# Weight loads and gate stores begun by ScalarE instead of SyncE, in a two-layer conv, mLSTM and latent-attention block

## The chip, the cores and the metric

The kernel runs on one NeuronCore of a Trainium2 chip. The core has a matrix engine (TensorE, PE in the profile, with its weight loads as PEld), a vector engine (VectorE, DVE), an engine for activations (ScalarE, ACT), a general one (GpSimd, POOL) and SyncE (SP), which computes nothing and here begins the DMA transfers. Each engine takes its own instructions strictly in order and waits on semaphores for the others. Every DMA runs on the same 16 DMA engines, whoever began it. The metric is the time of one execution on the device, in microseconds (us); 0.2% of it is about 5 us.

## What is computed

Two layers of a block with three branches over 512 tokens of width 1024 and 256 context tokens; the last layer needs the 512 tokens alone. In short:

```python
u = x * (1 + sc1) + sh1                       # modulation: silu(c) @ w_mod + b_mod, six parts
a, qkv, o_pre, g_if, cq, ckv, kr, gates = split(u @ w_in + b_in)   # the context likewise
y_conv = silu(layer_norm(depthwise_conv31(val * sigmoid(gate)))) @ w_conv_out
y_ml   = (sigmoid(o_pre) * norm(mlstm_bidirectional(q, k, v, g_if))) @ w_mlstm_out  # chunks of 128
y_mla  = attention(latent queries, latent keys and values, rope) @ w_mla_out        # 8 heads
g_a, g_b, g_c = split(sigmoid(gates))
y = (g_a * y_conv + g_b * y_ml + g_c * y_mla) @ w_out + b_out
x = layer_norm(alpha * x + g1 * y)
x = layer_norm(alpha * x + g2 * (relu(x' @ w1 + b1) ** 2 @ w2 + b2))   # x' modulated again
```

All numbers are float32.

## The kernel before, in words

Activations lie features by tokens: eight tiles of 128 x 768 (512 tokens and 256 of the context; 512 in the last layer). A product of float32 precision is made of three matmuls of a narrower float32 kind (fp32r): every operand is split into a high part (the rounded value) and a low part (the rest), and `mm3` (L265 to L268) adds high x high, high x low and low x high in PSUM. L268 is the only one of the three that reads a weight's low part. `gemm` (L279) runs this over the 128-row blocks of one weight tile; its result lies in one of two PSUM buffers (pg), and is taken out by ScalarE or VectorE.

A weight tile is 128 x 1024 (512 KB), up to 1152 wide. `wload` (L256) loads it into a buffer wr, ScalarE casts it to the high part wh (L261), and VectorE, or GpSimd for the gates and the output gate, subtracts to make the low part wl (L262). Each of wr, wh and wl has three buffers. So the load of tile i needs the wr buffer of tile i-3, free when that tile's low part is made, and the cast of tile i needs the wh buffer of tile i-3, free when its last matmul has run. `plan` (L201) lists the tiles of the whole kernel in the order of use, 328 of them, and `wget` (L249) hands out the next and calls `ahead` (L242), which keeps two more staged (LOOK = 2).

The stages of a layer: the convolution's inputs and its 31 taps on VectorE (L494), woven into what follows; value and gate columns (L536 to L538); the scans for the mLSTM's gates; keys and queries; the mLSTM chunk by chunk in both directions (`mstep`, with the decay weights loaded by L662 from a copy in DRAM, m_dram); the three branches' gates (24 tiles, L757 to L779), each put through tanh by ScalarE (L760) and stored to z_dram by L779; meanwhile pieces of the next modulation (`mod_pieces`, L151), whose w_mod tiles are loaded by L160, summed on VectorE (L165, into mda) and transposed by TensorE (L173). Then `merge` for the convolution and the mLSTM, which reloads each gate (`mload`, L76, into ml), multiplies it with the product (L803) and stores it again (L807); the latent projections; attention (scores, exponentials, transposes L982, values L1003); the third merge (L1065); w_out in token groups of 256 columns (L1103), whose residual comes by L1091 and is added in L1104, each group followed by a layer normalization (`ln_fm`: transposes L314 and L336, scaling L326) with its outputs L1080 to L1083; and the feed-forward part in eight blocks, where w1's results go through L1126 to L1129 and w2's are added in L1139. At the start, `first_loads`, `first_mods`, `first_u`, `first_w` and `first_gemm` (L360 to L399) weave the first modulation's w_mod loads (L130), the inputs' loads (L364) and three tiles of w_in; TensorE's order is written out by hand there alone.

Elsewhere the builder sets each engine's order when the program is built: it plans the instructions on assumed durations, by the order in which the code makes them and by when their operands and buffers are free. An edge of the kind `tc.add_manual_dep(..., NOSYNC)` only fixes an order and adds no wait on the chip where both instructions are on one engine. The builder puts in the semaphores as well. Before the change every DMA of the kernel is begun by SyncE, in one queue.

Of the kernel before, what the change touches and what calls it, by code (L numbers as in the profile page):

```python
# [14 lines left out]
NOSYNC = mybir.DependencyInfo(mybir.DependencyClass.NoSync, mybir.DependencyReason.DATA)  # L15
# [29 lines left out]
def build(tc, I, out):  # L45
    nc = tc.nc
    V, A, G, PE = nc.vector, nc.scalar, nc.gpsimd, nc.tensor
# [10 lines left out]
    def slot(name, dt=F32):  # L58
        return gp.tile([128, T], dt, name=name, tag="s")
# [13 lines left out]
    def mload(src):  # L73
        n = src.shape[1]
        t = mp.tile([128, 512], F32, name="ml", tag="m")
        nc.sync.dma_start(t[:, :n], src)  # L76
        return t[:, :n]
# [164 lines left out]
    def ahead(k):  # L242
        while len(staged) < k:
            p = next(todo, None)
            if p is None:
                return
            staged.append((p[0], wload(*p[1:])))

    def wget(*key, look=LOOK):  # L249
# [3 lines left out]
        ahead(look)  # L253
        return w

    def wload(src, n, eng):  # L256
        r = wp.tile([128, 1152], F32, name="wr", tag="wr")
        nc.sync.dma_start(r[:, :n], src)
        h = wp.tile([128, 1152], F32R, name="wh", tag="wh")
        lo = wp.tile([128, 1152], F32R, name="wl", tag="wl")  # L260
        A.copy(h[:, :n], r[:, :n])  # L261
        eng.tensor_sub(lo[:, :n], r[:, :n], h[:, :n])  # L262
        return h, lo

# [75 lines left out]
    def ln_fm(src, nk, groups, emit, base=0):  # L340
        for _ in ln_groups(src, nk, groups, emit, base):
            pass
# [3 lines left out]
    def pull(k):  # L346
        for _ in range(k):
            next(mods, None)
# [3 lines left out]
    z_dram = dp.tile([3, 8, 128, T], F32, name="z_dram")  # L352
# [100 lines left out]
    for l in range(L):  # L453
        full = l < L - 1
        n = T if full else S
# [44 lines left out]
        def some_taps(k):  # L500
            for _ in range(k):
                next(taps, None)

        for j in range(4):
# [5 lines left out]
            h = slot("hc")  # L510
# [15 lines left out]
        for hf, w_n in ((0, VG0), (1, VG1)):  # L526
            ws = [wget("w_vg", l, hf * 2 + q) for q in range(2)]
            for tt in range(NT):
                ps = pg()
                t0 = tt * 128  # L530
                for k in range(8):
                    wh, wl = ws[k // 4]
                    a, b = (k % 4) * w_n, (k % 4 + 1) * w_n
# [41 lines left out]
        for tt in range(NT):  # L575
            a, b = tt * 128, tt * 128 + 128
# [180 lines left out]
        def gate(b, mt):  # L757
            ps = win(MT_G + b * 8 + mt, n)
            t = slot("gt_")
            A.activation(t[:, :n], ps[:, :n], AF.Tanh, bias=HB(MT_G + b * 8 + mt), scale=0.5)  # L760
            return t
# [14 lines left out]
        for b in range(3):  # L776
            for mt in range(8):
                g = gate(b, mt)
                nc.sync.dma_start(z_dram[b, mt, :, :n], g[:, :n])  # L779
                some_taps(3)  # L780
                pull(2)
                if b * 8 + mt == 10:
                    some_taps(200)
                    ln_fm(ca, 4, groups, conv_emit)
# [105 lines left out]
        for hf in range(2):  # L890
            w = wget("w_ukv", l, hf)
            for tt in range(NT):
                ps = pg()
                t0 = tt * 128
                for k in range(2):
                    a, b = k * 512, (k + 1) * 512
# [21 lines left out]
        for hf in range(2):  # L918
            ws = [wget("w_uq", l, hf * 2 + q) for q in range(2)]
            for tt in qts:  # L920
                ps = pg()
                t0 = tt * 128
                for k in range(6):
                    wh, wl = ws[k // 3]
                    a, b = (k % 3) * 384, (k % 3 + 1) * 384
# [131 lines left out]
        for mp2 in range(4):  # L1057
            w = wget("w_ao", l, mp2)
            for i in range(2):
                mt = 2 * mp2 + i  # L1060
                ps = gemm(w, 4 * i, 4, oT, n)
                for (_, _, c0, c1), zz in zip(tg_, zg):
                    g = mload(z_dram[2, mt, :, c0:c1])
# [49 lines left out]
        for f in range(NF):  # L1113
            hid = []
            for j in range(FB):
                mt = f * FB + j
# [7 lines left out]
                r, hh, hl = slot("r"), slot("hidh", F32R), slot("hidl", F32R)  # L1124
# [7 lines left out]
            if f < NF - 1:  # L1132
                for mp2 in range(4):
                    w = wget("w2", l, f, mp2)
                    for i in range(2):
                        mt = 2 * mp2 + i
# [157 lines left out]
```

## Time and profile before

| | before |
|---|---|
| time, median of 3 runs | 2557.14 us (2556.3 to 2558.33) |
| the profiled execution's own time | 2557.35 us |
| its span, first to last instruction | 2555.5 us |
| mean granted TensorE clock | 0.993 |
| busy: TensorE, VectorE, ScalarE, GpSimd | 2470.4, 1580.6, 939.5, 298.7 us |
| DMA: all of it in one queue | 296.00 MB, 36.9% of 16 engines |
| mean rate over the span | 116 GB/s |

The profile is one execution. A row of its groups gives line, engine, operation, what is written and read, and how often; then the busy time, the mean of one in ns, and the engine's idle time just before, with what ended it. A row of waits gives who waited for whom: total us, times, longest. A row of windows gives a stretch of time, then the busy time of PE, PEld, DVE, ACT and POOL in it with counts, the granted clock as a share of full speed, the DMA engines' busy share and GB/s. A row of the timeline gives start, duration, engine (a q behind the name is its instruction queue), line, operation and tiles; neighbours of a kind are merged (x3), and a bracket holds the idle time before it and what ended it. DMA-issuing instructions do not count as busy time of an engine.

### The profile page before, as it was taken

Reading aid. Unit: us, or ns where it says so; the run is one execution under the profiler, and the core shown is the slowest. Engines: PE = TensorE matmul, PEld = TensorE weight load, DVE = VectorE, ACT = ScalarE, POOL = GpSimd, SP = SyncE. Lnnn points to the kernel's source line nnn. Section 1 sums busy time; section 2 is a strip of 40 time slices with the busy share of each in tenths; the row PEclk is TensorE's granted clock in tenths of the full one; section 3 lists DMA queues with packets and bytes.
Section 4 is the critical chain, followed back from the end, with each engine's and each line's share of the span. In section 5 each row is a group of like instructions: output and inputs, shape, how many; then the busy total and the mean of one; then the engine's idle time right before and its main releaser. Section 6 shows DMA issues by size and latency. Waiting matters only on the chain.

```text
span 2555.5 us, 38339 instructions
## 1 busy us (share of the span) xinstructions
PE 2470.4 (97%) x15272; PEld 2163.8 (85%) x15272; DVE 1580.6 (62%) x2847; ACT 939.5 (37%) x1607; POOL 298.7 (12%) x235
## 2 busy tenths in 40 slices
PE   7899989999999999999999999999999999999997
PEld 5888878888888899888888888977888888888887
DVE  4999976363356777655554379996043567554456
ACT  3123323222457563222222253333324575432323
POOL 0002132203000021000000031023411001100002
PEclk9999999999999999999999999999999999999999
DMA  7122344466110654343342252233563106333333
GB/s 264 53 75 70 98 163 161 166 195 210 62 34 1 188 168 142 122 131 115 108 129 88 65 149 78 59 106 101 175 203 111 50 18 213 101 99 92 99 94 113
DMA packets 137235, 298.45 MB, mean 117 GB/s; under 512 B 13776, under 2 KB 55248, under 8 KB 137056
## 3 DMA queue, kind: packets, MB, share of 16 engines
q1 hardware_dynamic: 137056, 296.00, 36.9%
q8 instruction: 120, 1.97, 0.3%
q14 instruction: 59, 0.48, 0.1%
HBM read 265.49 MB, written 30.46 MB: 116 GB/s over the span
## 4 chain that ended last, share of the span: by engine, by line
PE 81%; DVE 9%; DMA 4%; ACT 2%; issue 2%; POOL 1%; SPq 0%; DVEq 0%; ACTq 0%; POOLq 0%
PE pg L266 21%; PE pg L267 21%; PE pg L268 21%; PE pt L1003 2%; PE pt L982 2%; PE pt L266 2%; PE pt L267 2%; PE pt L268 2%; DVE ca L494 2%; DMA wm<-w_mod 1%; DMA ml<-z_dram 1%; PE pg L536 1%; PE pg L538 1%; PE pg L537 1%; DVE st L315 1%
## 5 line engine op out<-in xcount | busy, mean ns | idle before, releaser
L261 ACT CAST wh<-wr 128x1024 fp32r<-128x1024 f32 (+1 forms) x328 | 345.6, 1055 | 1202.4 <-PE pg L267 825.5
L262 DVE TENSOR_TENSOR wl<-wr,wh 128x1024 fp32r<-128x1024 f32 (+2 forms) x272 | 338.6, 1246 | 410.1 <-ACT wh L261 406.3
L268 PE MATMUL pg<-uh,wl 128*128 128x512 f32 (+1 forms) x1280 | 456.3, 356 | 2.2 <-DVE wl L262 2.2
L266 PE MATMUL pg<-uh,wh 128*128 128x512 f32 (+1 forms) x1280 | 457.2, 357 | 1.2 <-ACT gt__17278 L760 1.2
L267 PE MATMUL pg<-ul,wh 128*128 128x512 f32 (+1 forms) x1280 | 455.5, 356 | 0.7 <-POOL ul L1171 0.6
L266 PE MATMUL pg<-hidh,wh 128*128 128x512 f32 (+1 forms) x832 | 285.4, 344 | 3.9 <-DVE mv L318 2.0
L267 PE MATMUL pg<-hidl,wh 128*128 128x512 f32 (+1 forms) x832 | 284.9, 342 | 0.0
L268 PE MATMUL pg<-hidh,wl 128*128 128x512 f32 (+1 forms) x832 | 284.2, 342 | 0.0
L266 PEld LDWEIGHTS pg<-uh,wh 128*128 128x128 f32 x1280 | 244.2, 191 | 35.4 <-issue 2.5
L268 PEld LDWEIGHTS pg<-uh,wl 128*128 128x128 f32 x1280 | 243.9, 191 | 34.4 <-DVE wl L262 2.7
L267 PEld LDWEIGHTS pg<-ul,wh 128*128 128x128 f32 x1280 | 244.1, 191 | 33.2 <-POOL ul L1171 1.0
L494 DVE SCALAR_TENSOR_TENSOR ca<-hc,cols,ca 128x511 f32<-128x511 f32 (+9 forms) x360 | 227.8, 673 | 2.4
L262 POOL TENSOR_TENSOR wl<-wr,wh 128x1024 fp32r<-128x1024 f32 x56 | 145.7, 2602 | 562.6 <-ACT wh L261 562.6
L267 PE MATMUL pg<-u2l,wh 128*128 128x512 f32 (+1 forms) x608 | 210.3, 347 | 0.3 <-POOL u2l L1082 0.2
L1139 DVE SCALAR_TENSOR_TENSOR acc<-pg,mod,acc 128x512 f32<-128x512 f32 (+1 forms) x168 | 106.0, 659 | 168.6 <-PE pg L268 168.6
L268 PE MATMUL pg<-u2h,wl 128*128 128x512 f32 (+1 forms) x608 | 210.1, 347 | 0.0
L266 PE MATMUL pg<-u2h,wh 128*128 128x512 f32 (+1 forms) x608 | 209.9, 347 | 0.0
L165 DVE SCALAR_TENSOR_TENSOR mda<-wm,sil,mda 128x512 f32<-128x512 f32 x224 | 176.2, 808 | 7.6 <-DMA wm<-w_mod 5.0
L266 PEld LDWEIGHTS pg<-hidh,wh 128*128 128x128 f32 x832 | 157.3, 190 | 25.3 <-issue 3.5
L321 POOL TENSOR_TENSOR rs<-rs,mhalf 128x1 f32<-128x1 f32 x30 | 24.4, 819 | 1298.5 <-DVE rs L320 1298.5
L267 PEld LDWEIGHTS pg<-hidl,wh 128*128 128x128 f32 x832 | 157.9, 190 | 18.7 <-DVE hidl L1129 1.6
L268 PEld LDWEIGHTS pg<-hidh,wl 128*128 128x128 f32 x832 | 157.7, 189 | 18.0
(359 smaller groups left out, 4754.1 us busy)
## 6 DMA issues: line engine op xcount, KB each, us to landing
wr<-w SPq DMA_DIRECT2D x140, 512.0 KB, 3.6
wr<-w_in_fm SPq DMA_DIRECT2D x104, 512.0 KB, 3.8
wm<-w_mod SPq DMA_DIRECT2D x192, 256.0 KB, 4.5
wr<-w_out SPq DMA_DIRECT2D x40, 512.0 KB, 3.9
ml<-z_dram SPq DMA_DIRECT2D x104, 128.0 KB, 2.8
ml<-z_dram SPq DMA_DIRECT2D x48, 256.0 KB, 4.4
z_dram<-ml SPq DMA_DIRECT2D x32, 256.0 KB, 4.5
dm<-m_dram SPq DMA_DIRECT2D x20, 256.0 KB, 4.4
```

The costliest lines, as they stand in the source:

```text
L165: ins = V.scalar_tensor_tensor(av[v], w, sil[:, k, v:v + 1], av[v], op0=OP.mult, op1=OP.add)
L261: A.copy(h[:, :n], r[:, :n])
L262: eng.tensor_sub(lo[:, :n], r[:, :n], h[:, :n])
L266: PE.matmul(ps, hs, xh, start=first, stop=False)
L267: PE.matmul(ps, hs, xl, start=False, stop=False)
L268: return PE.matmul(ps, ls, xh, start=False, stop=last)
L315: V.bn_stats(st[:, hf * 6:(hf + 1) * 6], ps)
L494: V.scalar_tensor_tensor(acc[:, a:b], h[:, a + d:b + d], wd(15 + d), acc[:, a:b], op0=OP.mult, op1=OP.add)
L536: PE.matmul(o, uh[:, t0:t0 + 128], wh[:, a:b], start=(k == 0), stop=False)
L982: PE.transpose(p2[:, y * 128:(y + 1) * 128], P[:, (k4 + y) * 128:(k4 + y + 1) * 128], ident)
L1003: PE.matmul(po[64 * i:64 * i + 64, :256], va[B_.k0 + k][:, h * 64:h * 64 + 64], B_.pts[i][k // 2][:, k % 2, :], start=(k == 0), stop=(k == ...
L1139: V.scalar_tensor_tensor(acc[mt][:, c0:c1], ps[:, c0:c1], mc[:, 40 + mt, v:v + 1], acc[mt][:, c0:c1], op0=OP.mult, op1=OP.add)
```

## The change

Three edits. `wload` keeps a list of the casts; the load of a weight tile is begun by ScalarE (`nc.scalar`) instead of SyncE, with an edge that puts it behind the cast of the tile two before it, where there are two casts already; and the gates' stores (L779 before) are begun by ScalarE as well. All other DMAs, those of w_mod, m_dram, the reloads and the merged gates' stores among them, stay with SyncE.

```diff
+    casts = []
+
     def wload(src, n, eng):
         r = wp.tile([128, 1152], F32, name="wr", tag="wr")
-        nc.sync.dma_start(r[:, :n], src)
+
+        ld = nc.scalar.dma_start(r[:, :n], src)
+        if len(casts) > 1:
+            tc.add_manual_dep(ld.ins, casts[-2].ins.name, NOSYNC)
         h = wp.tile([128, 1152], F32R, name="wh", tag="wh")
         lo = wp.tile([128, 1152], F32R, name="wl", tag="wl")
-        A.copy(h[:, :n], r[:, :n])
+        casts.append(A.copy(h[:, :n], r[:, :n]))
         eng.tensor_sub(lo[:, :n], r[:, :n], h[:, :n])
         return h, lo
...
                 g = gate(b, mt)
-                nc.sync.dma_start(z_dram[b, mt, :, :n], g[:, :n])
+                nc.scalar.dma_start(z_dram[b, mt, :, :n], g[:, :n])
```

## The prediction, made before the result was known

> **What bounds the kernel now.** I read the profile page first: busy shares, then the chain that ended last.
>
> ```profile
> span 2555.5 us, 38339 instructions
> PE 2470.4 (97%) x15272; PEld 2163.8 (85%) x15272; DVE 1580.6 (62%) x2847; ACT 939.5 (37%) x1607; POOL 298.7 (12%) x235
> PE 81%; DVE 9%; DMA 4%; ACT 2%; issue 2%; POOL 1%; SPq 0%; DVEq 0%; ACTq 0%; POOLq 0%
> ```
>
> TensorE is busy for 2470.4 of 2555.5 us, so everything that is not matmul is 85.1 us. The change does not touch a matmul: all that it can win lies in those 85.1 us, and all that it can lose is new idle time of TensorE. So the next view is what TensorE waited for.
>
> ```profile
> PE pt L138 <- DMA wm<-w_mod: 10.4, 9, 4.0
> PE pt L173 <- DVE mda L165: 10.3, 3, 8.0
> PE pg L536 <- DVE gt L544: 6.9, 1, 6.9
> PE pg L266 <- DVE ml L803: 3.6, 2, 1.9
> PE pg L268 <- DVE wl L262: 2.9, 3, 2.2
> PE pg L266 <- DVE ml L1065: 1.4, 2, 1.2
> ```
>
> The columns are total us, times, longest. Only the first row is a wait for a DMA, and it belongs to the start. No row says that a matmul waited for a weight tile that was late from HBM; L262, which makes the tile's low part, cost 2.9 us in all. L803 and L1065 take reloaded gates (ml), which SyncE loads in a queue shared with the weights. A long wait has a tail, too, which the windows around two of them show (us, busy time and count of each engine, then granted clock, DMA share, GB/s):
>
> ```profile
> 171.00:178.00 7.00, 4.78 (x15) 3.45 (x14) 7.00 (x14) 1.83 (x2) 0.00 (x0) 0.76 0.30 91
> 328.00:340.00 12.00, 4.02 (x25) 2.13 (x25) 10.94 (x17) 1.60 (x3) 2.52 (x2) 0.76 0.63 195
> ```
>
> The granted clock is 0.76 there and 1.00 in undisturbed stages (two such windows stand below). At 0.76 over 7 us the clock took 0.24 x 7 = 1.7 us of TensorE's time after a wait of 2.2 us. In the second window most of the time at the low clock falls into the wait itself, where it costs nothing, so I put 1.7 us on each new or vanished wait from 2.2 us up.
>
> Next, SyncE's own waits:
>
> ```profile
> SPq L258 <- DVE wl L262: 1158.1, 219, 25.1
> SPq L258 <- POOL wl L262: 174.1, 47, 17.5
> SPq L130 <- DMA wm<-w_mod: 3.7, 13, 0.4
> ```
>
> SyncE stands for 1332.3 us in front of weight loads until the low part three tiles back is made (three wr buffers). Whatever is queued behind such a load waits too. The third row is a wait of one load for an earlier load of another tile: no data joins them, so it must be a shared completion semaphore. Loads can wait for unrelated transfers.
>
> **The weight loads, in the dense stages.** There is one load for each cast of L261, 328 by the first row below, and all leave SyncE for ScalarE. Load i now stands behind cast i-2; before, it went as soon as the low part of tile i-3 was made. The rows after it are from the feed-forward stage, and the last two give the median time to landing:
>
> ```profile
> L261 ACT CAST wh<-wr 128x1024 fp32r<-128x1024 f32 (+1 forms) x328 | 345.6, 1055 | 1202.4 <-PE pg L267 825.5
> 1156.96 17.05 SPq L258 DMA_DIRECT2D wr<-w  x3
> 1174.07 5.69 SPq L160 DMA_DIRECT2D wm<-w_mod  x7
> 1162.24 1.05 ACT L261 CAST wh<-wr 128x1024 fp32r<-128x1024 f32 x1 [7.31 <-PE pg L267]
> 1178.94 1.05 ACT L261 CAST wh<-wr 128x1024 fp32r<-128x1024 f32 x1 [7.28 <-PE pg L267]
> wr<-w SPq DMA_DIRECT2D x140, 512.0 KB, 3.6
> wr<-w_out SPq DMA_DIRECT2D x40, 512.0 KB, 3.9
> ```
>
> The two casts are two tiles apart, so a tile lasts 8.35 us here. A load begun behind the first (1163.3) lands 3.6 us later, at 1166.9; its cast starts at 1178.94. That is 12 us to spare, so here the later start costs nothing. What hides it is the two-tile lead; it would cost once two tiles last less than landing plus cast, 3.9 + 1.05 = 5 us.
>
> **The issue time.** On SyncE an issue took 328 ns for a load and 332 ns for a store:
>
> ```profile
> L258 SPq DMA_DIRECT2D wr<-w x140: 327/328/383, 949.4 to 2523.5; - x140
> L779 SPq DMA_DIRECT2D z_dram<-gt__2914 x1: 332/332/332, 272.9 to 272.9; - x1
> 415.00:545.00 130.00, 130.00 (x809) 114.14 (x808) 62.90 (x87) 30.10 (x36) 26.94 (x11) 1.00 0.48 161
> 938.00:947.00 9.00, 9.00 (x78) 8.86 (x76) 6.31 (x12) 9.00 (x20) 6.78 (x14) 1.00 0.18 60
> ```
>
> ScalarE gets 328 loads and 48 gate stores (24 in each layer), 376 x 0.33 = 124 us. No row shows an issue on ScalarE; the nearest is SyncE's, and I take it (from below, nothing; from above, twice that if the wait for its own tanh adds as much again). In the gate stage (the 130 us window) ScalarE is busy for 30.1 us beside a TensorE that never pauses: all of the stores and loads there are hidden. ScalarE is full only where the last group's normalization meets the next weights, 938 to 947: 9.00 of 9.00. The loads of the three tiles cast there move the casts by 3 x 0.33 = 1.0 us. Term: **+1.0** (0 to +5, if the other ends of token groups, where ScalarE is nearly as full, pay too: five groups of w_out x 1.0).
>
> **The w_out tiles.** Here a tile is 24 matmuls of 256 columns, 2.8 us at the rate of the 9 us window (78 matmuls in 9.00 us), and the two-tile lead shrinks to 5.6 us, just over the 5 us. One place is worse than the rest:
>
> ```profile
> 883.06 0.34 SPq L258 DMA_DIRECT2D wr<-w_out  x1
> 886.05 1.98 ACT L261 CAST wh<-wr 128x1024 fp32r<-128x1024 f32 x2
> 888.84 1.05 ACT L261 CAST wh<-wr 128x1024 fp32r<-128x1024 f32 x1
> 889.93 1.23 DVE L262 TENSOR_TENSOR wl<-wr,wh 128x1024 fp32r<-128x1024 f32 x1
> 891.33 0.48 DVE L1104 SCALAR_TENSOR_TENSOR t<-pg,g1h,xr 128x256 f32<-128x256 f32 x1 [0.17 <-PE pg L268]
> ```
>
> The load at 883.06 fills the tile cast at 888.84. After the change it stands behind the first cast of the pair (over by 887.1) and lands 3.9 us later, at 891.0: 2.2 us late. The low part then ends near 893.4 instead of 891.2, while the eviction at 891.33 shows TensorE ready for that tile by then. So up to 2.2 us of waiting; the tile's first matmuls need only the high part, so I take **+1.0** (0 to +2.2).
>
> **The start.** The first two loads have no edge to a cast and the fourth comes behind the second cast:
>
> ```profile
> 0.00:40.00 40.00, 27.27 (x307) 15.49 (x307) 16.05 (x36) 12.62 (x20) 1.80 (x18) 1.00 0.98 339
> 28.05 1.03 ACT L261 CAST wh<-wr 128x1024 fp32r<-128x1024 f32 x1
> 38.99 1.93 SPq L258 DMA_DIRECT2D wr<-w_in_fm  x3
> ```
>
> The 16 DMA engines are 0.98 busy at 339 GB/s for these 40 us. Loads 0 to 2 only move about within the stretch. But load 3, at 38.99 after everything urgent until now, is free to go at 29.1 and puts 512 KB in front of the last w_mod loads: 524288 B at 339 GB/s is 1.5 us, on the path. Term: **+1.5** (0 to +3.1, when load 4 gets in as well). The Trainium skill (DMA: Bandwidth & Descriptors, Queues, rings and completion order) says that each DMA engine takes turns between the queue rows it has work for, packet by packet; by that, ScalarE's load takes half of the engines while it lasts, which is the same 1.5 us.
>
> **What SyncE gains.** Off its queue go the waits of 1332.3 us. What stood behind them is mostly w_mod (the seven at 1174.07), which has whole tiles to spare, and reloads of ml. Of TensorE's waits, those for L803 and L1065, 3.6 + 1.4 = 5.0 us, end on reloads that shared a queue with 512 KB weight loads. But SyncE waits there for stores and semaphores too, and these stay, so I take a third: **-1.5** (-5.0 to 0). DVE in the mLSTM stage is the later party whether its loads come early or not: in the windows above it is busy 7.00 of 7.00 us and 10.94 of 12.00 us, so I put nothing on the waits for mda, gt and wl. The Trainium skill (DMA: Bandwidth & Descriptors, Issuing engines are not separate DMA queues) says that beginning DMAs on several engines saves only the sequencer's time for beginning them. By that rule this term is 0 and the time 1.5 us more; the trace here speaks against its letter, since SyncE's 1332.3 us are semaphore waits and not issue time, and these the other queue does take away.
>
> **Sum.** +1.0 +1.0 +1.5 -1.5 = +2.0 us. The profiled execution took 2557.35 us (span 2555.5), 0.2 above the median of the three runs, 2557.14. Against the median: 2559 us.
>
> **Rivals.**
>
> *ScalarE held up by a load (slower).* ScalarE works in order. A load that still has to wait for the low part three tiles back, or for a semaphore of an unrelated transfer, now holds casts and PSUM evictions. Where this would have happened in the old timing:
>
> ```profile
> 171.93 0.89 ACT L621 ACTIVATE kT<-pg,kb 128x768 f32<-128x768 f32 x1
> 177.83 1.21 DVE L262 TENSOR_TENSOR wl<-wr,wh 128x1024 fp32r<-128x1024 f32 x1
> 183.43 1.06 ACT L261 CAST wh<-wr 128x1024 fp32r<-128x1024 f32 x1 [10.60 <-PE pg L267]
> ```
>
> Behind the cast before 171.93 the load would wait until DVE's 177.83 + 1.21 = 179.0, about 7 us. Queued behind it are the kT eviction and the cast at 183.43. For it: DVE is the late engine in this stage and the instruction order is fixed at build time, so a place that fits the planned times need not fit the real ones. Against it: ScalarE was idle for 10.6 us just there, and TensorE has two PSUM buffers, one tile (8.35 us) of slack. It decides once a hold passes that slack or the eviction falls behind it: then a hold of 7.0 us becomes a wait of TensorE with its 1.7 us of clock, +8.7, 2559 + 8.7 = 2567.7 us.
>
> *A long wait dissolves (faster).* With SyncE free, w_mod and m_dram loads come earlier and the builder lays the instructions of the stages around the mLSTM anew. If that takes away the one wait of 8.0 us for mda with its 1.7 us of clock: 2559 - 9.7 = 2549.3 us. For it: SyncE spent 174.1 us before loads that wait for GpSimd, which makes the low parts in just this stage. Against it: DVE is the late engine there.
>
> *Nothing moves.* If all loads and stores keep to their old times within a tile, and the start's queue is as full as before, the terms vanish: 2557.1 us. This counts as no change, like the forecast.
>
> **How the numbers follow.** A measurement of this kernel tells apart about 0.2%, 5.1 us: 2552.0 to 2562.3. The forecast, with its terms between their bounds, gets 0.45 and "nothing moves" 0.10; both are no change, except for a tail of 0.05 in which the +5 of the issue time and the +3.1 of the start come together (2559 + 4.0 + 1.6 = 2564.6). The slower rival gets 0.22, the faster one 0.23. So faster 0.23, same 0.50, slower 0.27. The range reaches to the faster rival, 2549, and just past the slower, 2568; two holds or two vanished waits are left out.
>
> **What would show it.** In the changed profile: 376 issues on ScalarE's queue, wr issues right behind casts, no SyncE wait for wl; ScalarE's compute still 939 us and TensorE's 2470. Right if the wait for w_mod in the first 40 us has grown by about 1.5 us and the waits for ml have shrunk, while the waits for wl stay below 6 us. Wrong if ScalarE's own queue shows waits of several us at L258 with TensorE waiting for an eviction (the slower rival), or if the 8.0 us for mda is gone (the faster one). An issue on ScalarE of far over 0.33 us would break the second term.

## The result, and the profile after

The changed kernel takes 2588.64 us in the median of four runs (2583.74 to 2589.74), the kernel before 2557.73 us beside it. The ratio is 1.0114 with a 95% interval of 1.0100 to 1.0129. It is slower by 31 us by the medians and by 29 us by the ratio, where the forecast was 2 us and the range ended at 2568. The profiled execution has a span of 2586.0 us, 30.5 more than before. First the busy times and the two DMA queues of the page after:

```profile
span 2586.0 us, 38249 instructions
PE 2481.5 (96%) x15272; PEld 2172.5 (84%) x15272; DVE 1575.6 (61%) x2847; ACT 941.0 (36%) x1607; POOL 291.4 (11%) x235
q10 hardware_dynamic: 54144, 188.64, 23.5%
q1 hardware_dynamic: 82912, 107.36, 13.2%
```

The change did what it says: 188.64 MB go through a second queue (q10), and the bytes and each engine's count of working instructions are the same. Of the 30.5 us, TensorE is busy for 11.1 (2481.5 - 2470.4), in the same 15272 matmuls, so at a lower clock; the other 19.4 are idle time, 104.5 us after 85.1. Its waits after (total us, times, longest), of which the prediction showed the main ones of before:

```profile
PE pt L173 <- DVE mda L165: 11.7, 2, 8.2
PE pt L341 <- ACT ln L331: 7.8, 9, 3.0
PE pt L138 <- DMA wm<-w_mod: 7.3, 10, 1.6
PE pt L138 <- DVE wl L267: 7.1, 1, 7.1
PE pg L541 <- DVE gt L549: 6.9, 1, 6.9
PE pg L273 <- DVE wl L267: 6.1, 6, 2.7
PE pg L271 <- DVE ml L808: 6.0, 3, 3.9
...
PE pg L271 <- ACT wh L266: 5.3, 5, 1.9
```

Lines behind the edit are five further down than before (L266 is the cast, L267 the low part). The last row is new: matmuls wait for the cast of a weight tile, which no row of before shows. The wait for low parts (L273) has grown from 2.9 to 6.1 us, that for reloaded gates (L808) from 3.6 to 6.0, and at the start the waits for L138 are 7.3 + 7.1 us instead of 10.4. To see where, I compared stages with the same number of matmuls. This is the w_out stage of layer 0 after; the columns are those of the windows shown before (us, then busy time and count for PE, PEld, DVE, ACT and POOL; granted clock, DMA share, GB/s), and the second window lies inside the first:

```profile
869.00:983.00 114.00, 107.66 (x798) 102.26 (x796) 77.31 (x145) 63.22 (x109) 20.31 (x28) 0.96 0.61 190
949.00:956.00 7.00, 5.89 (x26) 4.75 (x26) 5.19 (x9) 6.57 (x17) 5.59 (x7) 0.66 0.00 0
```

And the same stage of the kernel before:

```profile
860.00:965.00 105.00, 102.92 (x797) 98.10 (x795) 76.86 (x144) 62.12 (x108) 20.67 (x28) 1.00 0.64 199
```

The same work took 114 us instead of 105. TensorE is busy for 4.7 us more of it (the clock is 0.96, and 0.04 x 114 = 4.6) and idle for 4.3 us more. The inner window points to the cause: for 7 us the DMA engines move nothing at all (0.00, 0 GB/s), in a stage that moves 190 GB/s on average, while ScalarE is busy for 6.57 of the 7. The timeline of ScalarE there (start, duration, engine, line, operation; ACTq is its instruction queue):

```profile
940.48 1.03 ACT L266 CAST wh<-wr 128x1024 fp32r<-128x1024 f32 x1
941.15 0.33 ACTq L261 DMA_DIRECT2D wr<-w_out  x1
...
946.28 2.78 ACT L331 ACTIVATE ln<-pt,rs 128x512 f32<-128x512 f32 x4 [1.20 <-DVE rs L327]
948.94 1.05 ACT L266 CAST wh<-wr 128x1024 fp32r<-128x1024 f32 x1
949.88 0.42 ACT L1086 CAST u2h<-uf 128x256 fp32r<-128x256 f32 x1
...
955.86 0.41 ACT L1086 CAST u2h<-uf 128x256 fp32r<-128x256 f32 x1 [0.41 <-DVE uf L1085]
955.87 0.33 ACTq L261 DMA_DIRECT2D wr<-w_out  x1
956.18 0.56 ACT L1088 ACTIVATE acc<-pt,ab,ag 128x256 f32<-128x256 f32 x1
956.25 0.44 ACTq L261 DMA_DIRECT2D wr<-w_out  x1
959.47 1.04 ACT L266 CAST wh<-wr 128x1024 fp32r<-128x1024 f32 x1 [2.73 <-DMA wr<-w_out]
```

Between the load at 941.15 and the next at 955.87 no weight load leaves. In between stand the scaling and all but one of the 16 outputs of the normalization, and ScalarE works in order. The next cast waits 2.73 us for the data, and TensorE waits for the cast and then for the low part:

```profile
960.56 0.39 PE L271 MATMUL pg<-zp,wh 128*128 128x256 f32 x1 [1.50 <-ACT wh L266]
...
961.82 0.58 PE L273 MATMUL pg<-zp,wl 128*128 128x256 f32 x1 [0.76 <-DVE wl L267]
```

In this stage TensorE waits 2.4 us for casts and 2.1 us for low parts; before, it waited 0 and 0.7 us for them. Before, the two loads that correspond (tiles 93 and 94) left SyncE at 927.65 and 930.66, in front of the normalization. The first of them left when its buffer came free: the low part of tile 90 had ended at 927.62.

### The profile page after: what moved, and what is told of

Its sections match the earlier page's. It is cut to its first block, busy times and chain, and to the rows that moved or that the text cites. A ratio compares the mean times of both kernels' runs of the same rounds, so it can differ in the third digit from the quotient of the medians.

```text
span 2586.0 us, 38249 instructions
## 1 busy us (share of the span) xinstructions
PE 2481.5 (96%) x15272; PEld 2172.5 (84%) x15272; DVE 1575.6 (61%) x2847; ACT 941.0 (36%) x1607; POOL 291.4 (11%) x235
## 3 DMA queue, kind: packets, MB, share of 16 engines
q10 hardware_dynamic: 54144, 188.64, 23.5%
## 5 line engine op out<-in xcount | busy, mean ns | idle before, releaser
L266 ACT CAST wh<-wr 128x1024 fp32r<-128x1024 f32 (+1 forms) x328 | 345.7, 1055 | 1226.2 <-PE pg L272 1078.3
L267 DVE TENSOR_TENSOR wl<-wr,wh 128x1024 fp32r<-128x1024 f32 (+2 forms) x272 | 337.5, 1243 | 404.8 <-ACT wh L266 401.5
L273 PE MATMUL pg<-uh,wl 128*128 128x512 f32 (+1 forms) x1280 | 455.9, 356 | 2.7 <-DVE wl L267 2.7
L273 PE MATMUL pg<-hidh,wl 128*128 128x512 f32 (+1 forms) x832 | 282.5, 341 | 0.0
L273 PEld LDWEIGHTS pg<-uh,wl 128*128 128x128 f32 x1280 | 244.1, 191 | 35.5 <-DVE wl L267 3.3
L273 PE MATMUL pg<-u2h,wl 128*128 128x512 f32 (+1 forms) x608 | 210.1, 346 | 0.1
L267 POOL TENSOR_TENSOR wl<-wr,wh 128x1024 fp32r<-128x1024 f32 x56 | 146.8, 2622 | 558.9 <-ACT wh L266 545.3
L273 PEld LDWEIGHTS pg<-hidh,wl 128*128 128x128 f32 x832 | 156.9, 189 | 18.3
L326 POOL TENSOR_TENSOR rs<-rs,mhalf 128x1 f32<-128x1 f32 x30 | 18.9, 636 | 1310.3 <-DVE rs L325 1310.3
```

The costliest lines, as they stand in the source:

```text
L266: casts.append(A.copy(h[:, :n], r[:, :n]))
L273: return PE.matmul(ps, ls, xh, start=False, stop=last)
L326: G.tensor_tensor(rs[:, 0:1], rs[:, 0:1], mhalf[:, 0:1], op=OP.pow)
```

## The experiments

My theory after the result: **the loads come late**. A load on ScalarE does not leave when its buffer is free, but when ScalarE gets to it, and where a tile is short (2.8 us in w_out) the lead is used up. Against it stood as rivals: ScalarE's issue time (376 x 0.33 us), ScalarE held up by waiting loads, the gate stores, and a rearranged order (the builder plans all engines anew when ScalarE has more to do). Below, a difference in us is the ratio's, taken of 2557.5 us.

### The two halves of the change

**Loads without stores** (e_loads_only): the gate stores go back to SyncE.

```diff
-                nc.scalar.dma_start(z_dram[b, mt, :, :n], g[:, :n])
+                nc.sync.dma_start(z_dram[b, mt, :, :n], g[:, :n])
```

> The weight loads stay with ScalarE, the 48 gate stores go back to SyncE. Theory (loads late): the 31 us come from loads that stand in ScalarE's queue behind its other work, above all in the two w_out stages; the stores have nothing to do with it, so about 2588 us, with the w_out stage of layer 0 (cast 76 to cast 104) still some 9 us longer than before. Rival (stores): each store makes ScalarE wait for its own tanh and delays evictions; then most of the 31 us goes, below 2570 us. Rival (rearranged order): the builder lays the gate and merge stages anew, so that the time moves by up to 10 us in either direction in those stages, with the w_out stages unchanged.

Measured: 2584.58 us, ratio 1.0109 (1.0092 to 1.0126). The loads alone cost 28 us.

**Stores without loads** (e_stores_only): the load in `wload` is SyncE's again, without the edge.

```diff
-        ld = nc.scalar.dma_start(r[:, :n], src)
-        if len(casts) > 1:
-            tc.add_manual_dep(ld.ins, casts[-2].ins.name, NOSYNC)
+        nc.sync.dma_start(r[:, :n], src)
```

> Only the 48 gate stores are begun by ScalarE, the weight loads stay with SyncE. Theory (loads late): the stores cost ScalarE 48 x 0.33 = 16 us beside a TensorE that does not pause there, so 2557 us within 5 us. Rival (stores): a good part of the 31 us is already here, above 2570 us. Rival (rearranged order): a few us in the merge stage (540 to 617 us), where the gates are read back.

Measured: 2562.22 us, ratio 1.0012 (1.0003 to 1.0022), 3 us. The rival of the stores falls as an explanation of the 31 us.

### The w_out loads, one way and the other

e_wout_on_sync takes the 40 loads of w_out out of the change. e_wout_only leaves nothing else in it: the comparison is turned round, and the gate stores are SyncE's.

```diff
+        if key[0] != "w_out":
             ld = nc.scalar.dma_start(r[:, :n], src)
             if len(casts) > 1:
                 tc.add_manual_dep(ld.ins, casts[-2].ins.name, NOSYNC)
+        else:
+            nc.sync.dma_start(r[:, :n], src)
```

> As the changed kernel, but the 40 loads of w_out go back to SyncE; the other 288 loads and the stores stay with ScalarE. Theory (loads late): the w_out stages lose their waits for the cast and the low part, 9 us in layer 0 and 5 us in layer 1, so about 2575 us, and a cast of w_out starts several us after its load has landed again (median 5.5 us before, 0.4 us in the changed kernel). Rival (issue time alone): 40 x 0.33 = 13 us of ScalarE's time leave, of which only a few us were on the path, 2584 us or more. Rival (rearranged order): the loss stays where it was or turns up elsewhere, about 2588 us.

> The reverse: only the 40 loads of w_out are begun by ScalarE, each behind the cast of the tile two back; the other 288 and the stores stay with SyncE. Theory (loads late): the w_out stages get their 9 and 5 us, so 2557 + 14 = 2571 us (2566 to 2576), the rest of the profile as before. Rival (issue time alone): 2557 to 2561 us. Rival (rearranged order): the 14 us are not here, but the order of the mLSTM and merge stages differs again, 2557 to 2565 us.

Measured: 2574.23 us, ratio 1.0061 (1.0046 to 1.0076), and 2570.25 us, ratio 1.0053 (1.0036 to 1.0071). These 40 loads of 328 cost about 14 us, nearly half of the loss, and both kernels fell where the theory put them. The window over the w_out stage of layer 0, with the same matmuls as the 105 us before and the 114 us after, first of e_wout_on_sync, then of e_wout_only:

```profile
868.00:973.00 105.00, 102.72 (x797) 98.05 (x795) 76.56 (x143) 61.66 (x108) 20.36 (x27) 1.00 0.65 203
```

```profile
862.00:977.00 115.00, 106.64 (x798) 101.07 (x797) 77.55 (x145) 62.97 (x109) 20.20 (x28) 0.97 0.59 184
```

With SyncE the stage has its old length and clock, with ScalarE it has the whole loss.

### Lateness without issues, issues without lateness

Two kernels hold the two explanations apart. In **e_late_sync** ScalarE issues nothing; one load of SyncE waits until the normalization is done.

```diff
-        nc.sync.dma_start(r[:, :n], src)
+        ld = nc.sync.dma_start(r[:, :n], src)
+        if key[0] == "w_out":
+            nout[0] += 1
+            if nout[0] == 20:
+                tc.add_manual_dep(ld.ins, late[0].ins.name, SYNC)
...
-            A.activation(acc[k][:, c0:c1], ps, AF.Identity, bias=ab2[:, k, v:v + 1], scale=ag[:, k:k + 1])
+            late[0] = A.activation(acc[k][:, c0:c1], ps, AF.Identity, bias=ab2[:, k, v:v + 1], scale=ag[:, k:k + 1])
```

> The kernel before, with one added wait: the load of tile 93 (w_out, layer 0, last group, tile 3), still begun by SyncE, waits until ScalarE has done the last normalization activation of the group before. ScalarE issues nothing. Theory (loads late): the lateness alone costs; TensorE waits at tiles 93 and 94 for the cast and the low part as in the changed kernel, and casts 92 to 99 drift by about 6 us, so 2563 us (2561 to 2566). Rival (issue time on ScalarE or the split over two queues): nothing of this is present, 2557 us, within 2.

Measured: 2564.55 us, ratio 1.0031 (1.0020 to 1.0043), 8 us. The stage and the wait of TensorE:

```profile
858.00:970.00 112.00, 104.84 (x799) 100.16 (x798) 76.96 (x144) 62.89 (x109) 20.23 (x28) 0.97 0.60 187
```

```profile
PE pg L273 <- ACT wh L268: 5.0, 1, 5.0
```

The load that waits also holds those behind it in SyncE's queue, so that those of tiles 93 to 95 leave within 1 us of each other, from 941.95 on:

```profile
941.95 7.62 SPq L261 DMA_DIRECT2D wr<-w_out  x5
```

One load is made late, two more with it, and the stage is 112 us long (with two matmuls more) at a clock of 0.97. Lateness is enough.

For the reverse, **e_dummy** adds to the kernel before a small store for each weight tile, begun by ScalarE, that nothing waits for (the list of casts is kept as in the change).

```diff
         nc.sync.dma_start(r[:, :n], src)
+        i = len(casts)
+        d = nc.scalar.dma_start(dq[i].rearrange("(p o) -> p o", o=1), ones)
+        if i > 1:
+            tc.add_manual_dep(d.ins, casts[-2].ins.name, NOSYNC)
```

> The kernel before, with one more DMA per weight tile: ScalarE begins a store of 128 x 1 numbers to unused memory, behind the cast of the tile two back, where the changed kernel has its weight load; all loads and stores stay with SyncE. It adds 328 issues to ScalarE that nothing waits for. Theory (loads late): ScalarE's issue time is hidden, 2557 us within 5 us, and the two w_out stages keep their length. Rival (issue time): most of the 31 us appear, above 2575 us, with the w_out stage of layer 0 several us longer.

Measured: 2813.62 us, ratio 1.0996 (1.0969 to 1.1022). This is more than either expected, and the reason is not the issue time: the page of e_dummy (us from issue to landing) shows that the stores slowed all other transfers.

```profile
wr<-w SPq DMA_DIRECT2D x140, 512.0 KB, 9.1
...
dq<-ones ACTq DMA_DIRECT2D x328, 0.5 KB, 8.9
```

A weight load lands after 9.1 us instead of 3.6. So the run says nothing of the issues, and **e_dummy2** repeats it with 16 rows of 512 B in place of 128 rows of 4 B:

```diff
-        d = nc.scalar.dma_start(dq[i].rearrange("(p o) -> p o", o=1), ones)
+        d = nc.scalar.dma_start(dq[i], dz[0:16, :])
```

> As e_dummy, with a store that moves 16 rows of 512 B instead of 128 single numbers, because the 128 rows of 4 B slowed every other transfer (a weight load landed after 9.1 us instead of 3.6). Again ScalarE begins 328 stores that nothing waits for, behind the cast of the tile two back; all loads stay with SyncE. Theory (loads late): the issue time of 328 x 0.33 us is hidden, so 2557 us within 6 us, with the w_out stage of layer 0 (casts 76 to 100) as long as before within 2 us. Rival (issue time): above 2565 us, with the w_out stages longer.

Measured: 2560.75 us, ratio 1.0000 (0.9991 to 1.0009). The w_out stage:

```profile
861.00:966.00 105.00, 102.58 (x797) 98.25 (x797) 76.83 (x144) 61.49 (x108) 20.93 (x27) 1.00 0.65 202
```

ScalarE's 328 added issues are hidden, in w_out too. The rival of the issue time falls.

### The place in ScalarE's order

**Without the edge** (e_noedge):

```diff
-        if len(casts) > 1:
-            tc.add_manual_dep(ld.ins, casts[-2].ins.name, NOSYNC)
```

> The changed kernel without the ordering edge to the cast two back: the builder alone decides where ScalarE issues a load. Theory (loads late): a load becomes free only when the low part three tiles back is made, which is mostly after that cast, so the edge binds at few places; the loads still stand behind the normalization, and the time stays within 6 us of 2588. Rival (the edge makes the loads late): the w_out stages get their 14 us back, about 2574 us. Rival (ScalarE held by loads): without the edge loads stand ahead of casts and hold ScalarE, above 2600 us.

Measured: 2587.99 us, ratio 1.0117 (1.0102 to 1.0133), as with the edge. The edge is not what makes the loads late.

**Written further ahead.** e_wout_lead2 is e_wout_only with two loads fetched ahead of the casts.

```diff
-            staged.append((p[0], wload(*p[1:])))
+            p, r = raw.pop(0)
+            staged.append((p[0], wload(r, *p[2:])))
+        while len(raw) < 2 and fetch():
+            pass
```

> As e_wout_only (the 40 loads of w_out begun by ScalarE, the rest by SyncE), but each load is written two tiles further ahead of its cast in the program, so that one more of them stands in front of the normalization between two token groups; still three wr buffers, so the load after that one cannot move. Engine, issues and bytes are the same. Theory (position in ScalarE's order): the casts no longer start right when their load lands, and most of the 13 us of e_wout_only goes, 2559 to 2564 us. Rival (ScalarE's issues or the second queue as such): nothing changes, 2570 us.

Measured: 2572.96 us, ratio 1.0055 (1.0037 to 1.0074), a miss. The fetching ahead had moved SyncE's loads as well: TensorE's wait for w_mod at the start is 14.1 us there and that for ml 4.9, against 11.0 and 1.6 in e_wout_only. In **e_wout_lead2b** it is done for w_out alone:

```diff
-        while len(raw) < 2 and fetch():
+        while len(raw) < 2 and after[0] and after[0][0][0] == "w_out" and fetch():
```

> As e_wout_lead2, but only the loads of w_out are written two tiles further ahead; all others are written where they were. In e_wout_lead2 casts 75 to 100 took 5.8 us longer than before, in e_wout_only 10.2 us. Theory (position in ScalarE's order): the same 4 us or more are won in layer 0 and some 1 us in layer 1, with the other stages as before, so 2562 to 2566 us against 2570 of e_wout_only; what is left is the load that three wr buffers keep behind the normalization. Rival (ScalarE's issues or the second queue as such): 2570 us again.

Measured: 2564.18 us, ratio 1.0023 (1.0014 to 1.0032): 6 us lost instead of 14, with the same engine, issues and bytes. The stage, and ScalarE's timeline at the normalization:

```profile
863.00:973.00 110.00, 106.36 (x798) 100.86 (x797) 77.51 (x145) 62.05 (x108) 18.92 (x27) 0.97 0.61 192
```

```profile
933.83 0.33 ACTq L269 DMA_DIRECT2D wr<-w_out  x1
...
950.32 0.33 ACTq L269 DMA_DIRECT2D wr<-w_out  x1
950.72 0.42 ACTq L269 DMA_DIRECT2D wr<-w_out  x1
951.08 1.03 ACT L279 CAST wh<-wr 128x1024 fp32r<-128x1024 f32 x1
954.07 1.05 ACT L279 CAST wh<-wr 128x1024 fp32r<-128x1024 f32 x1 [1.95 <-DMA wr<-w_out]
```

One more load now stands in front of the normalization, so the cast at 951.08 no longer waits for its data; the next one, whose load three buffers keep behind, still waits 1.95 us. With engine, issues and bytes the same, the place in the order makes the difference.

### Where the rest went

Five kernels put only some of the loads on ScalarE, with the condition at the place of `key[0] != "w_out"` above and the stores with SyncE. The first eight (e_start_only), and the merge and latent stages (e_merge_only):

```diff
+        if len(casts) < 8:
...
+        if key[0] in ("w_co", "w_mo", "w_ukv", "w_uq") or key[0] == "fm" and MT_O <= key[2] < MT_G:
```

> Only the first 8 weight loads are begun by ScalarE; the rest, and the stores, stay with SyncE. Theory (start traffic): loads 0 to 2 begin at the start of the program and share the 16 DMA engines, which are full, with the first w_mod loads; 2.5 to 4 us are lost until cast 5, so 2560 us. Rival (no loss): 2557 us, since the same bytes have to come in the first 40 us anyway.

> Only the loads of the merge and latent stages (MT_O, w_co, w_mo, MT_CQ, MT_CKV, w_ukv, w_uq; tiles 44 to 69 and their like in layer 1) are begun by ScalarE. Theory (merge traffic): a weight load on the other queue takes the DMA engines at once beside the small reloads and stores of the merge, which used to be in front of it in one queue; TensorE waits longer for ml, and 4 to 8 us are lost between casts 48 and 68, so 2561 to 2565 us. Rival (order alone): the loss in this stage came from the order that the builder gives the stages in front of it; then it is not here, and 2557 us.

Measured: 2563.74 us, ratio 1.0013 (1.0003 to 1.0022), 3 us; and 2564.46 us, ratio 1.0020 (1.0010 to 1.0031), 5 us. In e_start_only TensorE waits longer for w_mod (10.4, 9, 4.0 before):

```profile
PE pt L138 <- DMA wm<-w_mod: 13.2, 7, 7.0
```

In e_merge_only the time is as expected, but its profile speaks against the theory. TensorE waits 2.1 us for ml (L811) there, against 3.6 us before and 6.0 us in the changed kernel. These are windows over the merge, of the kernel before, the changed one and e_merge_only:

```profile
545.00:612.00 67.00, 62.76 (x365) 54.19 (x364) 34.46 (x55) 7.40 (x8) 17.45 (x16) 1.00 0.84 263
```

```profile
545.00:617.50 72.50, 65.45 (x368) 55.85 (x367) 34.60 (x55) 8.44 (x9) 18.07 (x15) 0.98 0.82 263
```

```profile
546.90:615.50 68.60, 64.50 (x365) 55.43 (x363) 34.67 (x54) 8.47 (x9) 18.16 (x15) 0.98 0.85 276
```

The changed kernel takes 5.5 us more than before (with three matmuls more), e_merge_only 1.6. So the merge loads alone do not bring back what the changed kernel loses in this stage. What the 5 us of e_merge_only are made of, and what the merge loses in the changed kernel, stay open.

Between the layers (e_turn_only):

```diff
+        if key[0] == "w2" and key[2] == 7 or key[0] in ("fm", "w_vg") and key[1] == 1 and len(casts) < 180:
```

> Only the loads between the layers (w2 of the last block in both layers and the first ten tiles of layer 1) are begun by ScalarE. Theory (loads and casts change places with the normalization): the casts of layer 1's first tiles stand between the normalization's activations and TensorE waits for ln, as in the changed kernel, 3.5 to 5 us between casts 164 and 175, so 2561 us. Rival: the loss between the layers came from drift of earlier stages and is not here, 2557 us.

Measured: 2563.75 us, ratio 1.0014 (1.0004 to 1.0023), 4 us. The place is the one that the theory names. These windows hold the same 341 or 342 matmuls around the turn, of the kernel before, of e_turn_only and of e_dummy2; in the changed kernel they take 54.2 us:

```profile
1485.00:1535.10 50.10, 45.94 (x341) 41.57 (x340) 38.92 (x77) 30.18 (x52) 21.79 (x22) 1.00 0.56 164
```

```profile
1489.50:1544.20 54.70, 47.77 (x342) 43.23 (x340) 39.50 (x77) 31.08 (x54) 15.57 (x22) 0.91 0.46 144
```

```profile
1486.30:1537.70 51.40, 46.69 (x342) 42.29 (x340) 38.80 (x77) 30.82 (x54) 19.52 (x22) 0.97 0.54 163
```

In e_turn_only TensorE waits here for the normalization's scaling (ln) twice, 4.9 us in all, as in the changed kernel; before, it does not wait for it here. In e_dummy2, where all loads are SyncE's, it waits for it once, 3.2 us, and the window is 1.3 us longer than before, not 4.6. So a DMA in ScalarE's order brings back part of this wait even where no load is late. Whether the rest is the order or the lateness stays open.

The feed-forward without its last block (e_ffn_only), and nearly all loads that no run above blamed (e_rest_only; the feed-forward again, w_vg, w_uq, w_ao, keys, queries and gates; the eight w_uq and two of w_vg were in the runs above as well):

```diff
+        if key[0] == "w1" and key[2] < 28 or key[0] == "w2" and key[2] < 7:
...
+        if key[0] in ("w_vg", "w_uq", "w_ao") or key[0] == "fm" and (MT_K <= key[2] < MT_O or key[2] >= MT_G) or key[0] == "w1" and key[2] < 28 or key[0] == "w2" and key[2] < 7:
```

> Only the feed-forward loads (w1 of tiles 0 to 27 and w2 of blocks 0 to 6, in both layers) are begun by ScalarE, behind the cast two back; everything else is with SyncE as before. Theory (loads late): in these stages a load has more than 7 us to spare between landing and cast, so 2557 us within 3 us. Rival (two queues as such): the start, merge and mLSTM stages profit or lose by a freer SyncE, and the time leaves this band.

> Only the loads that no other experiment blamed are begun by ScalarE: K, q and gate tiles of w_in, w_vg, w_uq, w_ao, and the feed-forward without its last block; the start, w_out, the merge, the tiles between the layers and all stores stay with SyncE. Theory (the losses are located): 2557 to 2562 us. Rival (a general cost of the second queue or of ScalarE's issues): a share of the 31 us by count of loads, some 200 of 328, above 2570 us.

Measured: 2559.15 us, ratio 1.0005 (0.9997 to 1.0014), and 2560.25 us, ratio 1.0003 (0.9993 to 1.0014). Some 200 of the 328 loads cost nothing that can be measured.

The parts by their ratios: w_out 14, merge 5, between the layers 4, start 3, gate stores 3, the rest 1, together 30 us against 29 us of the whole change (1.0114). Each part has an interval of about 2.5 us to either side (w_out 4.5). The parts are not quite a partition, either: w_uq and two w_vg tiles are in two of them, eight w1 tiles in none. And the profile of e_merge_only does not show its loss where the changed kernel has its own. So that the sum closes is partly luck. The share of w_out, nearly half, is the one that its stage and its two runs show alike. No version was found that is faster than the kernel before.

## Why the prediction was wrong

**The step that failed** is the term of the w_out tiles, +1.0 (0 to +2.2). The sum there, 5.6 us of lead against 5 of landing and cast, took it that a load goes right behind the cast two back. In its place the runs showed that a load leaves when ScalarE has done all that stands in front of it, and that this costs 9 us in the stage of layer 0 and 14 in both layers. At the place that I costed, the pair of casts at the start of the stage, TensorE waits 0.39 us for a cast and 0.65 for a low part, after 0.38 in all before, so my figure held there. The cost lies at the normalization between two token groups. One load left up to 14 us later than assumed: the buffer of tile 93 was free when the low part of tile 90 ended, at 940.35, and its cast two back ended at 941.51, but the load left at 955.87. The casts' wait for their data doubled; these are ScalarE's waits before, then after:

```profile
ACT wh L261 <- DMA wr<-w_out: 6.2, 4, 3.5
```

```profile
ACT wh L266 <- DMA wr<-w_out: 12.5, 9, 2.7
```

**The issue time (+1.0).** The place was named: "ScalarE is full only where the last group's normalization meets the next weights, 938 to 947: 9.00 of 9.00. The loads of the three tiles cast there move the casts by 3 x 0.33 = 1.0 us." The price of an issue was right as well (L261 on ScalarE's queue has a median of 334 ns). What was wrong is the direction. I asked what the loads do to a full ScalarE, and e_dummy2 says nothing that can be measured. I did not ask what a full ScalarE does to the loads. So no rival stood for lateness. Of my signs, only one touched it, that the waits for low parts stay below 6 us; they came to 6.1.

**The tail of a wait.** I put 1.7 us of clock on waits from 2.2 us up. In the w_out stage of layer 0, 4.7 of the 9 us are lost to the clock, though TensorE's longest wait there is the 1.50 us shown above. So shorter waits had a price that my range put at nothing. The bound fails in the other direction, too: in e_wout_on_sync TensorE waited 3.0 us for ml, and the clock is 1.00 from 558 to 568, through that wait and some 6 us behind it.

**The start (+1.5).** That more loads get into the full stretch was right, and the size is near the upper bound: I allowed 3.1 us if load 4 gets in as well, and it does. I had load 3 leave at 29.1, behind the second cast of the old timing. But the first loads no longer queue behind w_mod, the second cast starts at 6.88 instead of 28.05, and five loads leave within 16 us:

```profile
0.73 0.89 ACTq L261 DMA_DIRECT2D wr<-w_in_fm  x2
...
6.88 2.70 ACTq L261 DMA_DIRECT2D wr<-w_in_fm  x2
...
15.57 0.34 ACTq L261 DMA_DIRECT2D wr<-w_in_fm  x1
```

The first 307 matmuls took 42.5 us instead of 40, and e_start_only measured 3 us for it.

**What SyncE gains (-1.5).** SyncE did lose its waits for low parts (1158.1 + 174.1 = 1332.2 us; the prediction has 1332.3), and w_mod lands sooner (4.5 us before, 3.3 after, by the pages' DMA rows). But the wait for ml, from which I took the gain, rose from 3.6 to 6.0 us for L808 and fell only from 1.4 to 1.0 for L1070. At one place the two queues show it: a reload of ml leaves SyncE at 551.88 and a weight load leaves ScalarE at 551.89, so both move at once, where before the reloads had left at 548.32 and the weight at 551.30. I said that the trace spoke against the rule of the Trainium skill (DMA: Bandwidth & Descriptors, Issuing engines are not separate DMA queues), that a second issuing engine saves only the sequencer's time. The measured time agrees with the rule: 200 loads on a second queue won nothing (e_rest_only, 1.0003).

**What was not in the sum.** The gate stores were put at nothing because TensorE never pauses in the gate stage, and measured 3 us; what these are made of stays open. The place between the layers (4 us) had no term. I had counted a new order by the builder as a chance to win only.

**What was right.** The dense stages cost nothing, as their 12 us of spare time said (e_ffn_only). The faster rival did not come: the wait for mda is there with 8.2 us. The slower rival, ScalarE held up by a load's wait, names the other end of the same in-order queue, and was not it. Holds did occur, the longest of 5.1 us, by the row of ScalarE's semaphore waits before loads (duration min/median/max in ns):

```profile
L261 ACTq EVENT_SEMAPHORE  x130: 17/17/5115, 9.2 to 2161.4; - x130
```

But the median is 17 ns, and only three of the 130 are longer than that. The two longest, 5.1 and 1.9 us, begin at 76.7 and 93.4 us, in a stage that did not get longer: 910 matmuls in 156.5 us after (42.5 to 199), 916 in 157 us before (40 to 197).

## What to carry to other kernels

When a DMA is moved to an engine that computes, ask first what stands in front of it in that engine's order, and compare the longest such stretch with the lead of the buffer; the time that the issue takes from the engine comes second and was nothing here. A queue that is full of waits, as SyncE's was here, is doing its work: a load that waits at the head of a queue with nothing else to do leaves the moment its buffer is free, as that of tile 93 did before (927.62 and 927.65). Cost the move where tiles are shortest: here the 40 loads of w_out cost 14 us and some 200 others 1 us. And do not take the clock to stay up because every single wait is short.

## What the runs showed of the hardware

Stores of 128 rows of 4 B, only 0.19 MB in all, raised the median landing of the feed-forward's 512 KB loads from 3.6 to 9.1 us, and the busy share of the first queue from 36.9% to 69.6% for the same 296.00 MB (e_dummy); 16 rows of 512 B left it at 3.6 us and 37.0% (e_dummy2). The Trainium skill (DMA: Bandwidth & Descriptors, Specifications) says that transfers below 512 B are done by read-modify-write. These runs agree that 4 B rows cost far more than their bytes, and do not show the mechanism.

In the changed kernel the clock fell to a mean of 0.66 in the stretch from 949 to 956, in which TensorE's longest single wait was 0.50 us, in this row of its timeline:

```profile
950.05 0.38 PE L271 MATMUL pg<-zp,wh 128*128 128x256 f32 x1 [0.50 <-ACT wh L266]
```

In e_wout_only the same place has the same waits (0.49 us the longest) and no fall, as the first window below shows. The second shows the clock there after a wait of 2.96 us, which ended at 953.37:

```profile
942.50:949.50 7.00, 5.68 (x40) 4.51 (x40) 5.37 (x9) 7.00 (x18) 5.15 (x7) 1.00 0.00 0
952.00:961.00 9.00, 6.87 (x32) 6.67 (x33) 3.72 (x4) 4.18 (x4) 0.00 (x0) 0.62 0.66 213
```

With the wait of 3.0 us at a clock of 1.00 in e_wout_on_sync, the length of the longest single wait does not tell in these runs whether the clock falls. What decides it they do not show.
